# A two-block transformer step: Bst written in pieces from ScalarE's queue, constants moved, heads and skip later, zero products, four last pieces

## The chip, the cores and the metric

The kernel runs on one core of a Trainium2 chip. The metric is the device time of one execution in microseconds (us). One core has TensorE (PE, matrix products; PEld is its weight load), VectorE (DVE), ScalarE (ACT), GpSimd (POOL) and SyncE (SP), which here only issues DMA transfers. Each engine works through its own instructions in order; ACTq, SPq and POOLq are DMA issues from ScalarE, SyncE and GpSimd.

## What is computed

256 tokens of width 1024 go through two blocks. The first has two layers of attention (three kinds of heads) and a feed-forward part gated by a convolution over three tokens. The second runs a state-space scan (S5) and a sparse attention side by side, and then a product-key layer over 128 x 128 experts.

```
for layer in range(2):
    h = rms_norm(x, g_mix[layer])
    mix = concat(differential, moba, dilated attention of h @ w_in[layer])
    x = x + mix @ w_out[layer]
    u = causal_conv3(rms_norm(x, g_ffn[layer]) @ w_up[layer]) + conv_b
    gate, val = split(u)
    x = x + (silu(gate) * val) @ w_down[layer]
h = rms_norm(x, g_final)
proj = rmsnorm(h) @ w_in_2
y_ssm = gelu(real(C @ scan(a_bar, b_bar @ u)) + d_skip * u), then gated by w_glu
y_attn = softmax over the 64 keys that the index scores select
h = h + (sigmoid(g_ssm) * y_ssm @ w_ssm_up + sigmoid(g_attn) * y_attn @ w_attn_up) @ w_out
out = rmsnorm(h + experts(rmsnorm(h)))
```

## The kernel before

All large weights are cut into 515 tiles of 128 x 1024 numbers (512 KB each), and the class Weights (line 66) streams them. load_to issues a tile's transfer on SyncE's queue into one of four raw buffers. split_to cuts it into two parts, whi by ScalarE (line 94) and wlo = raw - whi by VectorE, now and then by GpSimd (line 96). TensorE makes three passes of each product from them (mm3: lines 156 and 159). There are six buffers for parts, and the splits run up to four tiles ahead.

The order of the work is written out by hand. Small work on ScalarE and VectorE is put off with w.post and issued by the next w.flush, which every request for a tile ends with, so that a posted step stands behind the splits of that request:

```
self.load_to(i + n + self.ahead)
self.split_to(...)
self.flush()
```

**Start.** build (line 1968) loads x and the first tiles on SyncE's queue. setup1 (line 333) loads five constants (mask_ab, masks, lamv, gd, cw) on GpSimd's queue; they are first used by the softmax steps from line 384 and the convolution. x is transposed on TensorE against the identity (line 217); ScalarE and VectorE evacuate it as hTh and hTl (lines 226, 228).

**Feed-forward part.** For each of 22 column blocks, j = 0 to 21, conv (line 774) runs on ScalarE (line 780) and VectorE (line 783) from a PSUM bank; tanh (line 790) follows on ScalarE, gated and split make gh and gl on VectorE, GpSimd and ScalarE (lines 796 to 804), each one flush later. Six blocks later down multiplies gh and gl with w_down. For j < 2 and for the last four blocks tanh is called at once, for the others it is posted.

**Beside it, in layer 0,** s5_b prepares the S5 tables as a generator that advances a step at a time between products. It makes BB on GpSimd, transposes it in eight groups of four (line 1020) into PSUM banks, posts eight evacuations into Bst (128 x 4096) on ScalarE, shown as L108, and writes all of Bst, 2 MB, to memory with one transfer on SyncE's queue (line 1026). Block 2 reads it back much later.

**Block 2.** A table plan, filled by at(m, step), says at which step m of the product loop each part is issued. UNITS gives m for the scores of the eight attention heads; the softmax (self.s3: VectorE lines 384 and 387, ScalarE line 390, TensorE line 399) follows two steps later, and values one more. The top-64 selection runs on VectorE before it (lines 1234 to 1239). scan is pushed through 11 levels on GpSimd and one on VectorE (lines 1269 to 1272); scan_end is a last push on VectorE. skip (line 1295, GpSimd) makes z = u * d_skip, which y_mm and gelu1 use from step 24 on. It is asked for at step 9.

**End.** The last products come out by columns of 128 in the order 4, 5, 0, 1, 2, 3, 6, 7. Each pair is copied by VectorE and ScalarE (lines 1944, 1946), and turn (line 1918) transposes it back one pair later; when a piece, (4, 6), (0, 4) or (6, 8), is complete, VectorE adds the residual (line 1931), ScalarE squares it and GpSimd scales it. Then come the sum of squares, the root and the output.

## Time and profile before

| what | value |
|---|---|
| median of 3 runs | 1671.91 us (1670.87 to 1672.17) |
| profiled execution | 1672.08 us, span 1670.0 us |
| mean granted clock of TensorE in the span | 0.988 of full speed |
| TensorE busy | 1616.1 us, 97% of the span |
| VectorE busy | 1299.8 us, 78% |
| ScalarE busy | 845.9 us, 51% |
| GpSimd busy | 699.0 us, 42% |
| moved by DMA | 328.49 MB, 197 GB/s in the mean |

The span runs from the first to the last instruction of the profiled execution; 2.1 us of its time lie outside it. A timeline row gives the start, the time, the engine, the line of the kernel, the operation, out<-in by the program's names with partitions x elements, and a count where like instructions in a row are drawn together; in brackets stands how long the engine had been idle before and what ended that. A matmul's time includes its way through the array, so that times of neighbours overlap. In the windows the clock is a share of 2.4 GHz, so 0.5 is the level of 1.2 GHz.

### The profile page before, as it was taken

How to read it: one execution, taken by the hardware profiler on the slowest of the kernel's cores; microseconds unless marked ns; L12 is line 12 of the kernel's file. 1: busy time of each engine (PE TensorE's matmuls, PEld its weight loads, DVE VectorE, ACT ScalarE, POOL GpSimd, SP SyncE). 2: the span in 40 equal slices, each digit the busy share in tenths (PEclk: the TensorE clock that was granted, in tenths of full speed). 3: DMA queues.
4: the chain of work that ended last, by engine and by line, in shares of the span. 5: the costliest groups of instructions: out<-in, count | busy, mean ns of one | idle time of the engine just before them, and what ended most of it. 6: DMA issues, size and time to landing. Idle time of an engine off the chain costs nothing.

```text
span 1670.0 us, 31715 instructions
## 1 busy us (share of the span) xinstructions
PE 1616.1 (97%) x12410; PEld 1476.5 (88%) x12410; DVE 1299.8 (78%) x2318; ACT 845.9 (51%) x1308; POOL 699.0 (42%) x610
## 2 busy tenths in 40 slices
PE   8999999889999999997999999999999999999996
PEld 6788999767889998775879999999999999999996
DVE  6775997666769866787663899889999889877775
ACT  6555655455556454643445545544444444455553
POOL 2313529322148933673020454323343222277773
PEclk9999999989999999998999999999999999999998
DMA  7435565464356557823356455777777655689982
GB/s 248 143 122 169 166 188 177 165 205 131 107 187 195 184 162 252 305 77 126 101 171 217 159 177 194 247 228 262 254 258 251 207 178 181 195 291 302 305 301 77
DMA packets 94325, 328.49 MB, mean 197 GB/s; under 512 B 11920, under 2 KB 16176, under 8 KB 93280
## 3 DMA queue, kind: packets, MB, share of 16 engines
q1 hardware_dynamic: 82992, 285.27, 51.1%
q0 software_dynamic: 10176, 39.03, 7.4%
q10 hardware_dynamic: 1008, 2.17, 0.4%
q8 instruction: 97, 1.59, 0.4%
q14 instruction: 52, 0.43, 0.1%
HBM read 318.57 MB, written 7.47 MB: 195 GB/s over the span
## 4 chain that ended last, share of the span: by engine, by line
PE 82%; DVE 8%; ACT 3%; DMA 3%; issue 2%; POOL 1%; ACTq 0%; SPq 0%; POOLq 0%; DVEq 0%
PE side L159 19%; PE acc L159 15%; PE side L156 10%; PE acc L156 8%; PE acc L1884 7%; PE acc L1877 6%; PE acc L1882 3%; PE acc L1879 3%; DVE wlo L96 3%; DMA raw<-in_ws 3%; PE side L1757 2%; ACT whi L94 1%; PE side L399 1%; PE side L376 1%; PE side L375 1%
## 5 line engine op out<-in xcount | busy, mean ns | idle before, releaser
L96 DVE TENSOR_TENSOR wlo<-raw,whi 128x1024 fp32r<-128x1024 f32 x462 | 609.2, 1330 | 221.0 <-ACT whi L94 220.3
L94 ACT ACTIVATE whi<-raw 128x1024 fp32r<-128x1024 f32 x511 | 535.8, 1057 | 456.1 <-PE acc L1882 174.0
L159 PE MATMUL side<-hTh,wlo 128*128 128x224 f32 (+1 forms) x1664 | 224.4, 277 | 2.8 <-DVE wlo L96 2.5
L156 PE MATMUL side<-hTh,whi 128*128 128x224 f32 (+1 forms) x1664 | 225.5, 278 | 0.8 <-ACT Bst L108 0.8
L159 PE MATMUL side<-hTl,whi 128*128 128x224 f32 (+1 forms) x1664 | 223.6, 277 | 0.0
L156 PEld LDWEIGHTS side<-hTh,whi 128*128 128x128 f32 x1664 | 207.6, 191 | 4.0 <-ACT Bst L108 1.1
L159 PEld LDWEIGHTS side<-hTh,wlo 128*128 128x128 f32 x1664 | 205.7, 191 | 3.9 <-DVE wlo L96 3.3
L159 PEld LDWEIGHTS side<-hTl,whi 128*128 128x128 f32 x1664 | 205.9, 191 | 0.0
L96 POOL TENSOR_TENSOR wlo<-raw,whi 128x1024 fp32r<-128x1024 f32 x49 | 125.9, 2572 | 178.2 <-ACT whi L94 170.9
L1847 POOL TENSOR_TENSOR ahl<-S,ahl 128x224 fp32r<-128x224 f32 x125 | 123.4, 988 | 173.8 <-ACT ahl L1846 173.2
L1884 PE MATMUL acc<-ahl,wlo 128*128 128x224 f32 x992 | 130.9, 274 | 0.0
L156 PE MATMUL acc<-whi,hTh 128*128 128x512 f32 x384 | 124.2, 416 | 1.3 <-ACT whi L94 1.3
L1877 PE MATMUL acc<-ahl,whi 128*128 128x448 f32 x496 | 124.4, 372 | 0.7 <-ACT S L1772 0.7
L1884 PEld LDWEIGHTS acc<-ahl,wlo 128*128 128x128 f32 x992 | 120.7, 192 | 0.0
L159 PE MATMUL acc<-wlo,hTh 128*128 128x512 f32 x384 | 117.9, 400 | 1.2 <-DVE wlo L96 1.1
L159 PE MATMUL acc<-whi,hTl 128*128 128x512 f32 x384 | 117.9, 399 | 0.3 <-DVE hTl L222 0.3
L159 PEld LDWEIGHTS acc<-wlo,hTh 128*128 128x128 f32 x384 | 72.7, 190 | 20.7 <-DVE wlo L96 3.2
L797 POOL TENSOR_TENSOR th<-th,cv 128x256 f32<-128x256 f32 x44 | 47.6, 1082 | 103.0 <-DVE th L796 99.6
L783 DVE SCALAR_TENSOR_TENSOR cv<-side,cw,cv 128x254 f32<-128x254 f32 (+1 forms) x176 | 72.5, 472 | 22.3 <-ACT cv L780 22.3
L159 PEld LDWEIGHTS acc<-whi,hTl 128*128 128x128 f32 x384 | 72.9, 190 | 18.3 <-DVE hTl L222 0.8
L1877 PEld LDWEIGHTS acc<-ahl,whi 128*128 128x128 f32 x496 | 84.3, 190 | 5.2 <-issue 1.4
L1696 POOL DMA_INDIRECT rows<-in_un,eid x32 | 47.0, 1470 | 96.4 <-DVE rows L1705 94.3
(487 smaller groups left out, 2787.7 us busy)
## 6 DMA issues: line engine op xcount, KB each, us to landing
raw<-in_ws SPq DMA_DIRECT2D x259, 512.0 KB, 4.0
raw<-in_us SPq DMA_DIRECT2D x128, 512.0 KB, 3.9
raw<-in_vs SPq DMA_DIRECT2D x128, 512.0 KB, 4.2
dBst<-Bst SPq DMA_DIRECT2D x1, 2048.0 KB, 7.4
dCT<-CT SPq DMA_DIRECT2D x2, 1024.0 KB, 7.9
tg<-dBst POOLq DMA_DIRECT2D x1, 2048.0 KB, 9.4
gb<-in_g_ffn SPq DMA_DIRECT2D x2, 512.0 KB, 5.3
s5bc<-in_s5bc SPq DMA_DIRECT2D x2, 512.0 KB, 5.8
```

The source lines that it names most:

```text
L94: self.nc.scalar.activation(hi, t, AF.Copy)
L96: eng.tensor_tensor(lo, t, hi.bitcast(FT), op=OP.subtract)
L156: mm(ps, sh, mh, start=first, stop=False)
L159: mm(ps, sl if side == "s" else sh, ml if side == "m" else mh, start=False, stop=last and side == late)
L783: nc.vector.scalar_tensor_tensor(o[which][:, n:], p[which][:, :S - n], cw[which][:, 2 - n:3 - n], o[which][:, n:], op0=OP.mult, op1=OP.add)
L797: nc.gpsimd.tensor_tensor(th, th, o[1], op=OP.mult)
L1696: G.indirect_dma_start(out=r, out_offset=None, in_=table, in_offset=bass.IndirectOffsetOnAxis(ap=eid[:, n:n + 1], axis=0))
L1847: G.tensor_tensor(al, src, ah.bitcast(FT), op=OP.subtract)
L1877: mm(acc[k][:, 0:2 * N], wts[i][0][:, s], A[i], start=first, stop=False)
L1879: mm(column(k), wts[i][0][:, s], A[i][:, 0:N], start=first and k % 2 == 0, stop=False)
L1882: mm(column(k), wts[i][0][:, s], A[i][:, N:2 * N], start=False, stop=False)
L1884: mm(column(k), wts[i][1][:, s], A[i][:, 0:N], start=False, stop=last and i == len(A) - 1 and (k < 4 or k % 2 == 1))
```

## The change

- UNITS is raised, so that the heads of block 2 come up to two steps later.
- The five constants of setup1 are issued on ScalarE's queue.
- idle makes products of zeros with no reader: ten before the first transposes, three behind the first evacuation.
- In the feed-forward part tanh is posted for the last four blocks too, in both layers.
- Each evacuation of Bst is followed on ScalarE by the transfer of its 256 KB; the transfer of 2 MB on SyncE's queue is gone.
- skip is asked for at step 12.
- The last columns are turned in four pieces of two, in the midst of the next pair's products, and three of the four sums of squares are added up ahead of the last.

```diff
-UNITS = (20, 20, 21, 22.5, 23, 23.5, 24, 25)
+UNITS = (21.5, 22, 22.5, 23, 23.5, 24, 24.5, 25)
...
     def setup1(self):
         self.mask_ab = self.b1c.tile([128, 384], FT, name="mask_ab")
-        nc.gpsimd.dma_start(out=self.mask_ab, in_=a["masks"][:, 0])
+        nc.scalar.dma_start(out=self.mask_ab, in_=a["masks"][:, 0])
         msk = c.tile([128, 2, 384], FT, name="masks")
-        nc.gpsimd.dma_start(out=msk, in_=a["masks"][:, 1:3])
+        nc.scalar.dma_start(out=msk, in_=a["masks"][:, 1:3])
...
         lamv = c.tile([128, 2, 4, 32], FT, name="lamv")
         gd = c.tile([128, 2, 64], FT, name="gd")
         cw = c.tile([128, 2, 44, 4], FT, name="cw")
...
+    def idle(self, n):
+        ps = self.acc.tile([128, 512], FT, name="acc")
+        for _ in range(n):
+            self.nc.tensor.matmul(ps, self.zero[:, 0:128], self.zero, start=True, stop=True)
...
-            if j < 2 or j >= NJ - 4:
+            if j < 2:
                 tanh(j, o)
             else:
                 w.post(tanh, j, o)
...
+        def put(dst, ps, at):
+            nc.scalar.activation(dst, ps.rearrange("p (a b) -> p a b", b=128), AF.Copy)
+            nc.scalar.dma_start(out=self.spill["Bst"][:, at:at + 512], in_=dst.rearrange("p g m -> p (g m)"))
+
         for i in range(8):
...
-            self.w.post(nc.scalar.activation, Bst[:, ri, gp], ps.rearrange("p (a b) -> p a b", b=128), AF.Copy)
+            self.w.post(put, Bst[:, ri, gp], ps, 2048 * ri + 512 * h)
             yield
             if i in (0, 1, 7):
                 yield
-        nc.sync.dma_start(out=self.spill["Bst"], in_=Bst.rearrange("p r g m -> p (r g m)"))
...
-        at(9, skip)
+        at(12, skip)
...
-        pieces = [(4, 6), (0, 4), (6, 8)]
+        pieces = [(4, 6), (0, 2), (2, 4), (6, 8)]
...
             for k in ks:
                 v_mm(124, A, wts, [k], True)
+                if b and k % 2 == 0:
+                    turn(order[2 * b - 2])
+                    turn(order[2 * b - 1])
+            if b == 3:
+                V.scalar_tensor_tensor(v, ms[:, :, 0], EPS, ms[:, :, 1], op0=OP.add, op1=OP.add)
+                V.tensor_tensor(v, v, ms[:, :, 2], op=OP.add)
...
-            for k in order[2 * b - 2:2 * b] if b else ():
-                turn(k)
         turn(6)
         turn(7)
-        V.scalar_tensor_tensor(v, ms[:, :, 0], EPS, ms[:, :, 1], op0=OP.add, op1=OP.add)
-        V.tensor_tensor(v, v, ms[:, :, 2], op=OP.add)
+        V.tensor_tensor(v, v, ms[:, :, 3], op=OP.add)
...
+                zero = self.zero = self.tiny.tile([128, 512], BF, name="zero", bufs=1)
+                nc.vector.memset(zero, 0.0)
+                self.idle(10)
...
                 self.h_ready(0)
+                self.idle(3)
```

Three places show how the instructions stand. First ScalarE's order at the end of layer 0, before. Here cv, th and gh are the steps of a column block (line 780, 792, 803), whi a split, L108 the evacuation of Bst:

```order
L94 ACTIVATE whi<-raw 128x1024 x2
L803 ACTIVATE gh<-th 128x256
L780 ACTIVATE cv_3723<-side,cw 128x256
L780 ACTIVATE cv_3725<-side,cw 128x256
L792 ACTIVATE th<-cv_3723 128x256
L108 ACTIVATE Bst<-side 128x512 x2
L94 ACTIVATE whi<-raw 128x1024
L108 ACTIVATE Bst<-side 128x512 x2
L94 ACTIVATE whi<-raw 128x1024
L108 ACTIVATE Bst<-side 128x512
L94 ACTIVATE whi<-raw 128x1024 x2
L803 ACTIVATE gh<-th 128x256
```

and in the change, the same stretch (line numbers are shifted; DMA dBst is a piece's transfer):

```order
L94 ACTIVATE whi<-raw 128x1024 x2
L786 ACTIVATE cv_3741<-side,cw 128x256
L786 ACTIVATE cv_3743<-side,cw 128x256
L1023 ACTIVATE Bst<-side 128x512
L1024 DMA dBst<-Bst 128x512
L1023 ACTIVATE Bst<-side 128x512
L1024 DMA dBst<-Bst 128x512
L94 ACTIVATE whi<-raw 128x1024
L809 ACTIVATE gh<-th 128x256
L798 ACTIVATE th<-cv_3741 128x256
L1023 ACTIVATE Bst<-side 128x512
L1024 DMA dBst<-Bst 128x512
```

The two convolution steps no longer stand behind gh, tanh has moved from before the evacuations to behind the next gh, and each evacuation is followed by its transfer. On SyncE's queue the tiles now follow each other with no transfer of Bst between.

Second VectorE's order in block 2, from the last step of the selection (msel) to the first softmax step (L384), before:

```order
L1239 SCALAR_TENSOR_TENSOR msel<-msel,mask_ab 128x384
L96 TENSOR_TENSOR wlo<-raw,whi 128x1024 x2
L1269 TENSOR_TENSOR ya<-st,ap 128x480
L1270 TENSOR_TENSOR ya<-st,ap 128x480
L1271 TENSOR_TENSOR ya<-ya 128x480
L1272 TENSOR_TENSOR st<-st,ya 128x15x32
L96 TENSOR_TENSOR wlo<-raw,whi 128x1024
L384 ISA sm,mx<-side,msel 128x128
```

and in the change:

```order
L1249 SCALAR_TENSOR_TENSOR msel<-msel,mask_ab 128x384
L96 TENSOR_TENSOR wlo<-raw,whi 128x1024 x2
L1279 TENSOR_TENSOR ya<-st,ap 128x480
L1280 TENSOR_TENSOR ya<-st,ap 128x480
L1281 TENSOR_TENSOR ya<-ya 128x480
L1282 TENSOR_TENSOR st<-st,ya 128x15x32
L96 TENSOR_TENSOR wlo<-raw,whi 128x1024 x3
L390 ISA sm,mx<-side,msel 128x128
```

Three splits stand ahead of the first softmax step behind scan_end, where one stood.

Third ScalarE's queue at the start, between the evacuation of the second half of x and the first roots, before:

```order
L194 ACTIVATE squares,ms<-x 128x512 x2
L226 ACTIVATE hTh<-side,g_93 128x128 x8
L94 ACTIVATE whi<-raw 128x1024 x5
L194 ACTIVATE squares,ms<-x 128x512 x2
L280 ACT_TABLE_LOAD
L280 ACTIVATE sincos<-sc_r 128x48
```

and in the change:

```order
L194 ACTIVATE squares,ms<-x 128x512 x2
L226 ACTIVATE hTh<-side,g_106 128x128 x8
L94 ACTIVATE whi<-raw 128x1024 x4
L336 DMA mask_ab<-in_masks 128x384
L338 DMA masks<-in_masks 128x768
L342 DMA lamv<-in_lam 128x256
L346 DMA gd<-in_g_diff 128x128
L349 DMA cw<-in_conv 128x2x176
L94 ACTIVATE whi<-raw 128x1024
L194 ACTIVATE squares,ms<-x 128x512 x2
```

The five constants stand between the fourth and the fifth of these splits. On GpSimd they are gone.

## Rows read from the trace of the kernel before

**Rows 1.** The page: busy time of each engine, share of the span, instructions.
```profile
PE 1616.1 (97%) x12410; PEld 1476.5 (88%) x12410; DVE 1299.8 (78%) x2318; ACT 845.9 (51%) x1308; POOL 699.0 (42%) x610
```

**Rows 2.** Waits of TensorE over the whole span: total, times, longest.
```profile
PE side L399 <- ACT sm L390: 10.8, 1, 10.8
PE acc L156 <- ACT gh L803: 6.4, 1, 6.4
PE side L217 <- DMA ident<-in_ident: 5.4, 1, 5.4
PE side L1020 <- ACT th L792: 3.4, 1, 3.4
...
PE side L156 <- ACT Bst L108: 0.8, 1, 0.8
```

**Rows 3.** Windows: length, busy PE, PEld, DVE, ACT, POOL, PE clock, DMA share, GB/s.
```profile
5.00:15.30 10.30, 8.47 (x23) 6.12 (x24) 5.56 (x11) 5.12 (x11) 1.23 (x2) 1.00 1.02 359
```

**Rows 4.** Timeline of the first 30 us, TensorE, then ScalarE and its queue (ACTq).
```profile
14.44 1.01 PE L156 MATMUL acc<-whi,hTh 128*128 128x512 f32 x2
...
18.75 0.63 PE L156 MATMUL acc<-whi,hTh 128*128 128x512 f32 x2
19.21 0.62 PE L159 MATMUL acc<-wlo,hTh 128*128 128x512 f32 x2
...
0.90 0.38 ACTq L1984 DMA_DIRECT2D g<-in_g_col  x1
...
15.34 1.06 ACT L94 ACTIVATE whi<-raw 128x1024 fp32r<-128x1024 f32 x1 [3.53 <-DMA raw<-in_ws]
...
25.61 1.06 ACT L94 ACTIVATE whi<-raw 128x1024 fp32r<-128x1024 f32 x1 [2.00 <-DMA raw<-in_ws]
```

**Rows 5.** Windows around the last five transpose groups of layer 0, same columns.
```profile
316.70:320.20 3.50, 0.07 (x2) 0.07 (x2) 3.01 (x5) 1.80 (x5) 1.41 (x2) 0.84 0.28 111
320.20:326.00 5.80, 5.80 (x16) 4.70 (x17) 3.15 (x3) 3.77 (x6) 0.72 (x1) 0.51 0.00 0
333.00:339.30 6.30, 0.00 (x0) 0.00 (x0) 1.54 (x2) 2.42 (x3) 0.00 (x0) 0.75 0.86 337
339.30:346.50 7.20, 6.44 (x15) 4.74 (x16) 2.99 (x4) 1.45 (x4) 2.75 (x2) 0.51 0.49 147
```

**Rows 6.** Timeline of that stretch: ScalarE, VectorE, SyncE's queue.
```profile
317.01 0.42 ACT L803 ACTIVATE gh<-th 128x256 fp32r<-128x256 f32 x1 [0.96 <-POOL th L797]
...
336.57 1.06 ACT L94 ACTIVATE whi<-raw 128x1024 fp32r<-128x1024 f32 x1 [9.29 <-DMA raw<-in_ws]
...
315.18 2.88 DVE L96 TENSOR_TENSOR wlo<-raw,whi 128x1024 fp32r<-128x1024 f32 x2
318.37 1.65 DVE L783 SCALAR_TENSOR_TENSOR cv<-side,cw,cv 128x255 f32<-128x255 f32 x4 [0.31 <-ACT cv L780]
...
307.02 8.26 SPq L83 DMA_DIRECT2D raw<-in_ws  x4
327.31 0.33 SPq L1026 DMA_DIRECT2D dBst<-Bst  x1
327.76 12.81 SPq L83 DMA_DIRECT2D raw<-in_ws  x6
```

**Rows 7.** The page's DMA issues: KB each, us from issue to landing.
```profile
raw<-in_ws SPq DMA_DIRECT2D x259, 512.0 KB, 4.0
...
dBst<-Bst SPq DMA_DIRECT2D x1, 2048.0 KB, 7.4
```

**Rows 8.** Timeline of block 2 before the attention heads: GpSimd, then VectorE.
```profile
709.23 2.99 POOL L1295 TENSOR_TENSOR z<-u,s5d 128x1024 f32<-128x1024 f32 x1
...
762.01 4.47 DVE L96 TENSOR_TENSOR wlo<-raw,whi 128x1024 fp32r<-128x1024 f32 x2
```

**Rows 9.** Timeline of the last 15 us: TensorE, then ScalarE.
```profile
1659.35 0.53 PE L1924 MATMUL side<-ident,rows 128*96 128x128 f32 x3 [0.27 <-DVE hTh L1931]
...
1661.19 0.19 ACT L1932 ACTIVATION_READ_ACCUMULATOR S<-hTh 128x1 f32 x1
```

More of the change, by code (lines that the diff above doesn't have):

```diff
@@ L341, in setup1 @@
         lsrc = a["lam"]
-        nc.gpsimd.dma_start(out=lamv.rearrange("p a b c -> p (a b c)"),
+        nc.scalar.dma_start(out=lamv.rearrange("p a b c -> p (a b c)"),
                             in_=bass.AP(tensor=lsrc.tensor, offset=lsrc.offset, ap=[[0, 128], [1, 256]]))
@@ L345, in setup1 @@
         gsrc = a["g_diff"]
-        nc.gpsimd.dma_start(out=gd.rearrange("p a b -> p (a b)"),
+        nc.scalar.dma_start(out=gd.rearrange("p a b -> p (a b)"),
                             in_=bass.AP(tensor=gsrc.tensor, offset=gsrc.offset, ap=[[0, 128], [1, 128]]))
         cw = c.tile([128, 2, 44, 4], FT, name="cw")
-        nc.gpsimd.dma_start(out=cw.rearrange("p l a b -> p l (a b)"), in_=a["conv"].rearrange("l p n -> p l n"))
+        nc.scalar.dma_start(out=cw.rearrange("p l a b -> p l (a b)"), in_=a["conv"].rearrange("l p n -> p l n"))
         self.cw = cw
@@ L1913, in peer @@
         xg = [self.raw.tile([128, D], FT, name="raw") for _ in range(2)]
-        ms = self.tiny.tile([128, 2, 3], FT, name="ms3")
-        pieces = [(4, 6), (0, 4), (6, 8)]
+        ms = self.tiny.tile([128, 2, 4], FT, name="ms3")
+        v = self.tiny.tile([128, 2], FT, name="vars")
+        pieces = [(4, 6), (0, 2), (2, 4), (6, 8)]
         tok = [slice(0, 128), slice(0, N - 128)]
         def turn(k):
-            i = [k0 <= k < k1 for k0, k1 in pieces].index(True)
+            i = pieces.index((k // 2 * 2, k // 2 * 2 + 2))
             k0, k1 = pieces[i]
@@ L1948, in peer @@
                     V.tensor_tensor(dst, acc[k][:, N:2 * N], dst, op=OP.add)
-            for k in order[2 * b - 2:2 * b] if b else ():
-                turn(k)
         turn(6)
         turn(7)
-        v = self.tiny.tile([128, 2], FT, name="vars")
-        V.scalar_tensor_tensor(v, ms[:, :, 0], EPS, ms[:, :, 1], op0=OP.add, op1=OP.add)
-        V.tensor_tensor(v, v, ms[:, :, 2], op=OP.add)
+        V.tensor_tensor(v, v, ms[:, :, 3], op=OP.add)
         r = self.rsqrt(v, 2)
```

## The prediction

> **What bounds the kernel now.** I read the page first, then TensorE's waits, then windows over the stretches where it waited, then the timelines there. The page shows TensorE busy 97% of the span [rows 1]. So the other engines' loads matter only where TensorE stands still or runs at half its clock, and 1670.0 less 1616.1 leaves 53.9 us of standing still. The waits name the large pieces [rows 2]: 10.8 us for the first softmax of block 2, 6.4 us for gh at the end of layer 0, 5.4 us for the identity at the very start, 3.4 us at a transpose at the end of layer 0; outside that list stands the tail, where only the other engines work. The change touches all five. None of its parts removes TensorE work worth counting; it adds 13 small products and reorders the rest.
>
> Standing still has a second price. In the windows the granted clock is 0.51 while TensorE works off what a wait left behind [rows 5], which is the 1.2 GHz level in place of 2.4 GHz; a pair of 512-column products that lasts 0.63 us at full speed lasts 1.01 us [rows 4].
>
> **Head: constants and zero products, 2.0 us gained (0 to 2.7).** Up to 15.3 us the DMA share is 1.02 at 359 GB/s [rows 3], so what lands is a matter of bytes. ScalarE waits 3.53 us for the fourth weight tile and starts on it at 15.34 [rows 4]; TensorE can't go on without it. The five constants are 966,656 bytes by the shapes in the diff. Behind four more splits they no longer stand ahead of that tile: 0.967 MB / 359 GB/s = 2.7 us. That is the upper end. But up to 14.44 us TensorE is at the low level [rows 4], and would still be working through the first three tiles when the fourth lands at about 12.6; only the zero products, by bringing the clock up before the first transposes, let both come together. Neither part alone does much: zero products alone meet the same late tile, so I cost them at 0 by themselves. They run in the 5.4 us in which TensorE waits for the identity [rows 2]: ten single products of 0.23 us (half the 0.46 us from one pair to the next at full speed [rows 4]) at 0.51 of the clock are 4.5 us, which ends about when the identity lands; if the cover is too short, some tenths of delay. I take 2.0, because the transposes of the second token block and their evacuation don't shrink with the bytes. The lower end, 0, is that the constants give back later what they took. Their five issues at 0.38 us each [rows 4] are 1.9 us on ScalarE, in front of a split that now waits 2.00 us for its tile [rows 4]: hidden, unless the tile comes earlier by more than that. Their bytes now share with tiles that TensorE has several products in hand for.
>
> **End of layer 0: 13.5 us gained (5 to 15).** The 2 MB table Bst now leaves SyncE's queue with one transfer at 327.31, after the last evacuation; the queue had issued its last tile by 315.3 and six tiles stand behind the table [rows 6]. Their buffers came free with the splits that end at 318.06 [rows 6], so they waited 9.7 us for order alone. The first then lands so late that ScalarE waits 9.29 us for it, to 336.57 [rows 6]; gh stands behind that split on ScalarE, and TensorE behind gh. With the table in eight pieces on ScalarE's queue, tiles go out near 317 and 318 and land 4.0 us later [rows 7], ahead of the splits that want them. From the last transposes TensorE then has the work between 326.0 and 333.0 (the edges of windows in rows 5), 7 us; ScalarE needs one evacuation 0.6, one issue 0.4, two splits 2.1 and gh 0.4, together 3.5 us. So gh is there 3.5 us ahead, and the following subtraction on GpSimd too. Terms:
> - the wait for gh and the short one behind it: 6.3 + (7.20 - 6.44) = 7.1 us [rows 5];
> - the low clock behind it: 6.44 x (1 - 0.51) = 3.2 us [rows 5];
> - the wait of 0.8 us for an evacuation of Bst [rows 2], which now comes ahead of a split: 0.8 us;
> - the wait of 3.4 us at the seventh transposes [rows 2]: it ends with tanh of the last column block, behind gh at 317.01 and VectorE's four steps at 318.37 [rows 6]. With tanh posted, these steps still follow two splits that end at 318.06, so they can't move far; I keep 2.4 us of it and count 1.0;
> - the low clock behind that, (1 - 0.51) x 5.80 = 2.8 us [rows 5]. The clock of 0.84 over that wait means that it fell about 2.3 us in (0.32 of 3.5 us at half). [...]
> Together 13.5. With that clock kept it is 14.9, without 12.1. Against it stand eight issues of 0.38, 3.0 us of ScalarE in a stretch where it is busy about 3.8 of 5.8 us [rows 5]; if they fall where TensorE waits for a split, the gain sinks to about 5 (below).
>
> What decides at this place is the order of issue, not bandwidth: between 320.2 and 326.0 the DMA share is 0.00 while buffers are free [rows 5]. The Trainium skill speaks against both queue moves: "DMA: Bandwidth & Descriptors", section "Issuing engines are not separate DMA queues", says that transfers run on the same 16 engines whoever issues them, and that another issuer saves only the sequencer's issue time. By it the moves would save that time, 0.3 us, and the waits would stay; that case is the rival on the table's bytes.
>
> **Attention heads and skip: 1.2 us gained (-0.4 to 2.7).** The first pair of heads goes from 20 to 21.5 and 22, so at least 1.5 steps of the plan, six product pairs each, come ahead of the wait for the softmax: 1.5 x 6 x 0.46 us [rows 4] = 4.1 us. But VectorE has no idle time there, and its order now has two more splits ahead of the first softmax step: 2.88 us for two [rows 6]. Net 1.2. If only one of them delays the softmax it is 2.7. Against it, skip (2.99 us on GpSimd [rows 8]) now runs just behind the scan, beside VectorE's scan_end. What that costs is bounded by the two splits that ran beside the scan, 4.47 us [rows 8] against 2.88: 1.6 us at most, which makes -0.4. Skip's old place was already in GpSimd's idle time, so moving it saves nothing. I take 1.2, since VectorE's small steps are short beside a split. Most of the 10.8 us remains: the softmax still waits for VectorE.
>
> **Tanh in layer 1: 0.** The same chain there ended without a wait in TensorE's list [rows 2].
>
> **Last columns: 0.8 us gained (0.4 to 1.3).** Now the transposes of the last columns wait 0.27 us for VectorE and end near 1659.9, and ScalarE's squares run without a break until 1661.38 [rows 9]. In four pieces the last transposes start right behind their evacuation and only two narrow squares are left. Four earlier transposes move ahead of the last products (+0.4), the two wide squares and the wait fall off the path (-1.2).
>
> **Sum.** 2.0 + 13.5 + 0 + 1.2 + 0.8 = 17.5 us. The profiled execution took 1672.08 (span 1670.0), which gives 1654.6; the runs' median is 1671.91, 0.2 lower, which gives 1654.4. A measurement of this kernel tells a difference of about 0.2% (3.3 us) from none.
>
> **Rivals.**
> - *ScalarE becomes late at the end of layer 0.* Three microseconds of issues stand between evacuations and splits, each split feeds TensorE, and the wait for gh comes down only to 3.5 us with the low clock after it. The gain there is 13.5 - 3.5 - 3.2 - 1.4 = 5.4, the sum 9.4, the time 1662.5. For it: ScalarE is the engine that every wait there names. Against: the margin of 3.5 us. Chance 0.18.
> - *Head and heads give nothing.* The constants come back at 24 us on DMA engines that are still full, and take their 2.7 us from the tiles of the next products; skip costs VectorE all of the 1.6 us. Then 13.5 + 0.8 - 0.4 = 13.9, and 1658. Chance 0.17.
> - *Zero products raise nothing.* They end before the identity lands or leave the clock low; then the head gives some 0.5 in place of 2.0, and the time is 1656, inside the forecast's range.
> - *All upper ends:* clock kept at the seventh transposes, one split covered: 2.7 + 14.9 + 2.7 + 1.3 = 21.6, and 1650.3. Chance 0.05.
> - *The table's bytes hold the tiles back wherever they are issued.* The first tile behind the table landed near 336.5, 8.8 us after its issue, against 4.0 us for a tile at large [rows 6, 7], so sharing does slow it. If the pieces and the tiles share in the same way in the new place, for long enough to keep gh late, the 7.1 and 3.2 us stay: 17.5 - 10.3 = 7.2, and 1664.7. Against: 4.8 us more than 321 is 326, and gh 3.5 us later is still ahead of 333. Chance 0.03. (This is where the Trainium skill's rule, above, leads.)
> - *Slower: issues on ScalarE that block.* If each of the later seven issues has to wait for an earlier transfer's landing, 4.0 us [rows 7], ScalarE stands 28 us in a stretch of about 23, of which it now idles four tenths, some 9 us [rows 5]. TensorE then waits 19 us where it waits 3.4 + 7.1 now, so the end of layer 0 loses 8.5 in place of gaining 13.5: 17.5 - 13.5 - 8.5 = -4.5, and 1676. It decides from a mean wait of about 3.4 us for each issue. Against: the queue's issue at the start goes through in 0.38 us [rows 4], and the DMA engines are nearly idle there. Chance 0.05, of which 0.02 near the point that decides.
>
> **Chances.** Forecast 0.52; the rivals 0.18, 0.17, 0.05, 0.03 and 0.05. The range 1649 to 1664 takes in all but the last two. Faster by over 0.2%: 0.95; within: 0.02; slower: 0.03.
>
> **What would show it.** Right: no wait of TensorE for gh near 330, tiles issued by SyncE near 317, a clock of 1.00 through 330 to 345 in layer 0; the fourth tile's split near 12.7 and full-speed products before 10 us; a softmax wait in block 2 split in two and still 8 to 10 us in all; squares that end nearer to the last product. Wrong: ScalarE's queue standing at a piece of Bst, a wait for a split in front of a side product at 305 to 325, or a low clock that starts elsewhere.

## The result and the profile after

| | before | changed |
|---|---|---|
| median, six runs each | 1671.59 us (1668.09 to 1672.28) | 1650.8 us (1648.52 to 1660.29) |
| ratio to before, 95% interval | 1 | 0.9888 (0.9863 to 0.9913) |
| profiled execution, its span | 1672.08, 1670.0 us | 1649.52, 1647.6 us |
| mean granted clock in the span | 0.988 | 0.994 |

The change is faster by 20.8 us, or 1.1%. Forecast were 1654.4 us and a range of 1649 to 1664. Executions of the changed kernel spread further than those of before (the table's ranges), and the long ones show a lower mean clock, 0.990 against 0.995; where it fell in them is not shown. The mean clock and the busy time tell the same from two sides: on the page after, TensorE works 3.2 us less than before [rows 1] for 13 instructions more, and stands still for 34.7 us in place of 53.9.

```profile
PE 1612.9 (98%) x12423; PEld 1473.7 (89%) x12423; DVE 1296.5 (79%) x2322; ACT 846.9 (51%) x1312; POOL 697.4 (42%) x607
```

To see where the 22.4 us of the two spans came from, I cut each span at three places that every kernel here has: TensorE's transposes of the normalized rows (xn) of the second half of the tokens, ahead of the feed-forward part of layer 0, that of layer 1, and the experts. In the timeline of the changed kernel these are:

```profile
141.76 0.66 PE L217 MATMUL side<-ident,xn 128*128 128x128 f32 x4 [0.53 <-ACT xn L712]
...
460.20 0.66 PE L217 MATMUL side<-ident,xn 128*128 128x128 f32 x4 [0.52 <-ACT xn L712]
...
853.22 0.66 PE L217 MATMUL side<-ident,xn 128*128 128x128 f32 x4 [0.54 <-ACT xn L712]
```

The same rows of before start at 144.96, 481.54 and 876.65. The differences of these times are the lengths of the stages; the last column runs to the end of the span.

| kernel | to layer 0's feed-forward part | to layer 1's | to the experts | to the end | span |
|---|---|---|---|---|---|
| before | 144.96 | 336.58 | 395.11 | 793.35 | 1670.0 |
| changed | 141.76 | 318.44 | 393.02 | 794.38 | 1647.6 |
| difference | -3.2 | -18.1 | -2.1 | +1.0 | -22.4 |

The first stage holds the start, the second the end of layer 0, the third the attention heads of block 2, the fourth the tail. The profiles of the experiments below give the spread of a stage whose code is the same: 141.1 to 142.5 in the first, 318.15 to 318.7 in the second, 392.4 to 395.75 in the third, 792.5 to 795.3 in the fourth. So -2.1 in the third and +1.0 in the fourth are within what these stages vary by; the gains of the first and the second are beyond it, and most of the whole lies in the second.

TensorE's waits after (total, times, longest) no longer have gh, the transposes at the end of layer 0 and the evacuation of Bst [rows 2]. The wait for the identity is 0.2 in place of 5.4, with zero products running until then; that for the softmax is 2.8 in place of 10.8, with one of 2.5 for a split ahead of it (the longest in the first line). The 2.8 is one profile's: in the six others with the same steps in block 2 it is 0.3 to 5.4.

```profile
PE acc L159 <- DVE wlo L96: 5.7, 6, 2.5
...
PE side L405 <- ACT sm L396: 2.8, 1, 2.8
...
PE side L217 <- DMA ident<-in_ident: 0.2, 1, 0.2
```

Windows over the end of layer 0 (length, busy PE, PEld, DVE, ACT, POOL, PE clock, DMA share, GB/s) show 1.00 of the clock throughout, where rows 5 have 0.51 behind each wait, and a DMA share that never falls to 0.00:

```profile
300.00:310.00 10.00, 10.00 (x75) 9.35 (x74) 8.29 (x13) 8.52 (x14) 4.23 (x3) 1.00 0.82 278
310.00:320.00 10.00, 9.92 (x50) 7.96 (x49) 6.61 (x11) 7.99 (x14) 3.54 (x3) 1.00 0.98 338
320.00:330.00 10.00, 10.00 (x49) 8.14 (x48) 7.13 (x8) 5.64 (x10) 3.73 (x4) 1.00 0.66 211
```

The timeline there, ScalarE with its queue, then VectorE, then SyncE's queue:

```profile
310.39 1.00 ACT L786 ACTIVATE cv<-side,cw 128x256 f32<-128x256 f32 x2
311.28 0.59 ACT L1023 ACTIVATE Bst<-side 128x512 f32<-128x512 f32 x1
311.91 0.33 ACTq L1024 DMA_DIRECT2D dBst<-Bst  x1
312.28 0.60 ACT L1023 ACTIVATE Bst<-side 128x512 f32<-128x512 f32 x1 [0.40 <-ACT Bst L1023]
...
320.70 0.40 ACT L809 ACTIVATE gh<-th 128x256 fp32r<-128x256 f32 x1
...
312.06 1.64 DVE L789 SCALAR_TENSOR_TENSOR cv<-side,cw,cv 128x255 f32<-128x255 f32 x4
...
297.94 30.91 SPq L83 DMA_DIRECT2D raw<-in_ws  x13
```

A piece's issue takes 0.33 us and keeps ScalarE for 0.40 between two evacuations. SyncE's queue holds 13 tiles in a row with nothing between them. The last gh starts at 320.70 and TensorE has no wait for it. VectorE's four convolution steps (cv, L789) run at 312.06; before, the last ones ran at 318.37 [rows 6].

The start, TensorE, then ScalarE and its queue:

```profile
1.22 4.01 PE L376 MATMUL acc<-zero 128*128 128x512 bf16 x10 [1.22 <-DVE zero L1997]
...
8.27 0.73 PE L156 MATMUL acc<-whi,hTh 128*128 128x512 f32 x2
...
16.49 0.63 PE L156 MATMUL acc<-whi,hTh 128*128 128x512 f32 x2
...
12.42 1.06 ACT L94 ACTIVATE whi<-raw 128x1024 fp32r<-128x1024 f32 x1 [1.28 <-DMA raw<-in_ws]
...
19.56 0.34 ACTq L336 DMA_DIRECT2D mask_ab<-in_masks  x1
```

The ten zero products end just ahead of the identity, the first pair of weight products takes 0.73 us where pairs took 1.01 as late as 14.44 [rows 4], and the fourth split starts at 12.42 where it started at 15.34 [rows 4]. As a mark for the start I take the second whi pair behind the transposes of the second half of x: 16.49 here, 18.75 before [rows 4].

Block 2 ahead of the first softmax, TensorE, VectorE, GpSimd:

```profile
743.83 0.73 PE L159 MATMUL acc<-wlo,hTh 128*128 128x512 f32 x2 [2.50 <-DVE wlo L96]
...
753.80 0.84 PE L405 MATMUL side<-ident,sm 128*128 128x128 f32 x3 [2.84 <-ACT sm L396]
...
741.50 5.12 DVE L96 TENSOR_TENSOR wlo<-raw,whi 128x1024 fp32r<-128x1024 f32 x2
...
742.65 2.89 POOL L1305 TENSOR_TENSOR z<-u,s5d 128x1024 f32<-128x1024 f32 x1
```

The tail, TensorE's last product and the last transposes, which wait 0.89 us for the copies of its result:

```profile
1635.73 0.50 PE L1894 MATMUL acc<-S 128*128 128x224 f32 x3
1637.11 0.82 PE L1935 MATMUL side<-ident,rows 128*128 128x128 f32 x4 [0.89 <-DVE rows L1963]
```

From the last product's end (1636.23) to the span's end there are 11.4 us; before, the same stretch was 12.4 (1657.64 to 1670.0).

### The profile page after: what moved, and what is told of

Read it like the earlier page. It is cut to its first block, busy times and chain, and to the rows that moved or that the text cites. A ratio compares the mean times of both kernels' runs of the same rounds, so it can differ in the third digit from the quotient of the medians.

```text
span 1647.6 us, 31746 instructions
## 1 busy us (share of the span) xinstructions
PE 1612.9 (98%) x12423; PEld 1473.7 (89%) x12423; DVE 1296.5 (79%) x2322; ACT 846.9 (51%) x1312; POOL 697.4 (42%) x607
## 3 DMA queue, kind: packets, MB, share of 16 engines
q8 instruction: 97, 1.59, 0.4%
## 4 chain that ended last, share of the span: by engine, by line
PE 87%; DVE 4%; ACT 3%; DMA 2%; POOL 2%; issue 1%; ACTq 0%; DVEq 0%; POOLq 0%
PE side L159 22%; PE acc L159 16%; PE side L156 11%; PE acc L156 8%; PE acc L1894 7%; PE acc L1887 6%; PE acc L1892 3%; PE acc L1889 3%; PE side L1767 2%; DVE wlo L96 2%; DMA raw<-in_ws 1%; ACT whi L94 1%; PE side L405 1%; PE side L382 1%; PE side L381 1%
## 5 line engine op out<-in xcount | busy, mean ns | idle before, releaser
L96 DVE TENSOR_TENSOR wlo<-raw,whi 128x1024 fp32r<-128x1024 f32 x462 | 600.5, 1311 | 203.4 <-ACT whi L94 202.1
L789 DVE SCALAR_TENSOR_TENSOR cv<-side,cw,cv 128x254 f32<-128x254 f32 (+1 forms) x176 | 72.4, 472 | 21.5 <-ACT cv L786 21.5
```

Of the source, the lines that this page charges most:

```text
L96: eng.tensor_tensor(lo, t, hi.bitcast(FT), op=OP.subtract)
L789: nc.vector.scalar_tensor_tensor(o[which][:, n:], p[which][:, :S - n], cw[which][:, 2 - n:3 - n], o[which][:, n:], op0=OP.mult, op1=OP.add)
```

## The experiments

The theory: the second stage's 18.1 us come from two causes of about equal size, the table's place in the order of issue and tanh's place in ScalarE's order. The rivals: that the eight pieces do it by their size or early start, that bandwidth was short, that tanh is worth little, as forecast. For the other stages each part is undone alone.

**1. One transfer of 2 MB on SyncE's queue again**, rest as changed.

```diff
-            nc.scalar.dma_start(out=self.spill["Bst"][:, at:at + 512], in_=dst.rearrange("p g m -> p (g m)"))
...
+        nc.sync.dma_start(out=self.spill["Bst"], in_=Bst.rearrange("p r g m -> p (r g m)"))
```

> The changed kernel, but Bst leaves with one transfer of 2 MB on SyncE's queue at the end of the steps again. Theory (the order of issue held the tiles): the tiles of layer 0's end stand behind the table again, TensorE waits 4 to 8 us for gh and works the next 6 us at the low clock (3 us more), so 7 to 11 us slower than the changed kernel. Rival (the table's bytes share the 16 DMA engines wherever they are issued): within 2 us of the changed kernel, and no wait for gh.

Measured: 1659.41 us (1658.13 to 1660.6), ratio 0.9928 (0.9911 to 0.9944). The waits for gh (6.3) and gl (0.7) are back, the second stage is 328.13, 9.7 us longer. The timeline, SyncE's queue and ScalarE:

```profile
300.25 9.14 SPq L83 DMA_DIRECT2D raw<-in_ws  x5
316.85 0.33 SPq L1036 DMA_DIRECT2D dBst<-Bst  x1
317.30 12.79 SPq L83 DMA_DIRECT2D raw<-in_ws  x6
...
326.07 1.06 ACT L94 ACTIVATE whi<-raw 128x1024 fp32r<-128x1024 f32 x1 [9.24 <-DMA raw<-in_ws]
```

The queue issues its last tile by 309.4, then stands until the table goes at 316.85; the next tiles start at 317.30 and the split that needs the first waits 9.24 us for it (the bracket of 326.07). The low clock behind the wait is back too, in the window 328 to 336 (columns as in the windows above):

```profile
328.00:336.00 8.00, 6.42 (x16) 4.77 (x17) 3.69 (x5) 2.23 (x6) 2.76 (x2) 0.56 0.48 161
```

**2. One transfer of 2 MB, but on ScalarE's queue.** The same edit with nc.scalar for nc.sync.

> The changed kernel, but Bst leaves with one transfer of 2 MB on ScalarE's queue, after the last evacuation. Theory (order of issue): the tiles on SyncE's queue pass it, no wait for gh, within 1.5 us of the changed kernel. Rival (bytes): the tiles that go out from 319 us on land 4 to 5 us late, and TensorE waits 3 us or more there or just behind. If the pieces themselves matter (work for ScalarE in small steps), this kernel is faster by up to 1 us, since seven issues fall away.

Measured: 1650.25 us (1649.3 to 1662.94), 0.9908 (0.9874 to 0.9943); second stage 318.15, no wait for gh. Against experiment 1 only the queue differs, and the second stage is 10.0 us shorter; against the changed kernel only the pieces do, and it lies at the edge of the 318.2 to 318.7 of those with pieces. So the pieces don't matter, the queue does. The page's DMA issues (KB each, us from issue to landing) show that the table does share the DMA engines with the tiles:

```profile
dBst<-Bst ACTq DMA_DIRECT2D x1, 2048.0 KB, 9.9
```

It takes 9.9 us beside tiles where it took 7.4 [rows 7], and the tile issued at 318.97 landed 8.4 us later. Nobody waits for either.

**3. Tanh at once for the last four blocks again.**

```diff
-            if j < 2:
+            if j < 2 or j >= NJ - 4:
```

> The changed kernel, but tanh of the last four column blocks is called at once again in both layers. Theory: the wait at the seventh transposes hangs on the order in which tanh, the evacuations and VectorE's steps are asked for, so it comes back with 3 to 4 us, and the low clock behind it with 2 to 3 us: 5 to 7 us slower than the changed kernel. Rival (that wait went because the table and the queue went): no wait there, within 1 us. The prediction's own step (most of the wait is bound by VectorE's splits and stays) would have the two kernels differ by 1 to 2.4 us.

Measured: 1662.11 us (1658.81 to 1664.12), 0.9946 (0.9925 to 0.9967); second stage 326.21, 7.8 longer. TensorE waits 4.9 us at the seventh transposes, in two waits of 0.5 and 4.4 that the list puts down to tanh. ScalarE, VectorE, TensorE:

```profile
308.78 0.42 ACT L798 ACTIVATE th<-cv 128x256 f32<-128x256 f32 x1 [2.39 <-DVE cv L789]
...
314.26 1.00 ACT L786 ACTIVATE cv<-side,cw 128x256 f32<-128x256 f32 x2
317.63 0.42 ACT L798 ACTIVATE th<-cv 128x256 f32<-128x256 f32 x1 [2.37 <-DVE cv L789]
317.95 0.58 ACT L1023 ACTIVATE Bst<-side 128x512 f32<-128x512 f32 x1
...
316.29 1.64 DVE L789 SCALAR_TENSOR_TENSOR cv<-side,cw,cv 128x255 f32<-128x255 f32 x4
...
318.07 0.63 PE L1031 MATMUL side<-ident,BB 128*128 128x128 f32 x4 [4.37 <-ACT th L798]
```

ScalarE stands 2.39 us and then 2.37 us at tanh for VectorE's steps of the same block. What it has to do behind that, evacuations and splits and the next block's convolution, is late by as much: VectorE's last steps run at 316.29 in place of 312.06. The evacuation's wait of 0.8 is back, and the low clock (0.75 over 6.9 us from 318.1, 1.7 us) makes up nearly all of the rest of the 7.8. The medians differ by 11.3; what the second stage leaves lies in the third, 397.57 in this profile, where the clock is at 0.50 from 783.0 to 789.8.

The list names tanh because it ended last, but the times speak for VectorE. The transposes start 0.02 us behind tanh's end (318.05) and 0.14 behind the end of VectorE's fourth step (317.93); before, the second distance is 0.15 too (320.02 to 320.17). A wait for ScalarE alone ends 0.05 us behind it here. In five waits of other profiles, at the softmax's transposes, for both engines with ScalarE done 1.95 us earlier, TensorE starts 0.15 us behind VectorE's step. So TensorE waited for VectorE's four steps. Tanh, which needs the third of them, ends at nearly the same moment.

**4. The kernel before with tanh posted in layer 0 and 1, and nothing else.** The same line, the other way.

> The kernel before with one edit: tanh of the last four column blocks is posted. Theory (that edit alone takes the wait at the seventh transposes away): the waits of 0.8 and 3.4 us and the low clock of 2.8 us behind go, the wait for gh stays at 6 to 6.5 us with its low clock, so 6 to 8 us faster than before. Rival (it needs the pieces on ScalarE's queue as well): the wait of 3.4 us stays, within 2 us of before.

Measured: 1663.64 us (1661.42 to 1664.38), 0.995 (0.9933 to 0.9967); second stage 327.66, 8.9 shorter. The wait of 3.4 and the one of 0.8 for Bst are gone, the wait for gh stays at 6.4. The 8.9 of this run and the 9.7 of the first make 18.6, against 18.1 for the whole: two causes, nearly additive.

**5. No zero products**, the constants where the change has them.

```diff
-                self.idle(10)
...
-                self.idle(3)
```

> The changed kernel without the 13 products of zeros. Theory (zero products and constants only gain together): TensorE works up to 13 or 15 us at the low clock, the fourth tile is there near 12.4 us and waits for it; the first pass ends 1.5 to 2.2 us later, and so does everything. Rival 1 (zero products do nothing): within 0.5 us, clock low or not. Rival 2 (they are the whole gain of the head): 2.5 to 3 us slower.

Measured: 1653.16 us (1648.27 to 1658.58), 0.9906 (0.9882 to 0.993); first stage 143.09, 1.3 longer than changed. TensorE, then ScalarE:

```profile
13.99 1.05 PE L159 MATMUL acc<-whi,hTl 128*128 128x512 f32 x2
...
18.62 0.63 PE L156 MATMUL acc<-whi,hTh 128*128 128x512 f32 x2
...
9.88 3.05 ACT L94 ACTIVATE whi<-raw 128x1024 fp32r<-128x1024 f32 x3
```

The splits run without a wait, and TensorE is at the low level (1.05 us a pair) until 14.85: now TensorE is late, not the tile. Its mark stands at 18.62, 0.13 ahead of before. (In experiment 4, which has neither part, the clock rises by 12.2 all the same, TensorE then waits for the late tile, and the mark is 19.57.)

**6. The constants on GpSimd's queue again**, with the zero products (nc.gpsimd for nc.scalar in the five lines of setup1).

> The changed kernel with the five constants on GpSimd's queue at the start again. Theory: the fourth tile lands 2.5 to 2.9 us later, near 15.2 us, TensorE is warm but waits for it, 2.0 to 2.8 us slower, of which up to 1 us may come back because the tiles at 22 to 32 us no longer share with the constants. Rival (the constants only change places with later tiles): within 0.7 us.

Measured: 1653.93 us (1652.55 to 1655.74), 0.99 (0.9883 to 0.9917); first stage 144.13, 2.4 longer. TensorE's mark, and ScalarE's fourth split, late again:

```profile
18.70 0.62 PE L156 MATMUL acc<-whi,hTh 128*128 128x512 f32 x2
...
15.29 1.06 ACT L94 ACTIVATE whi<-raw 128x1024 fp32r<-128x1024 f32 x1 [3.37 <-DMA raw<-in_ws]
```

TensorE is at its full level and waits for the tile: 18.70, 0.05 ahead of before. In the ten profiles here that have both parts, the mark lies between 16.49 and 17.87, 17.17 in the mean; in the two that have neither, at 18.75 and 19.57 (before and experiment 4), 19.16 in the mean. So both together give 2.0 us, and neither alone, one profile each, comes near that; whether one alone gives nothing or half a microsecond, two profiles that differ by 0.8 can't tell. The change moves the constants in time and to another queue at once, and no run parts the two. The two latest marks with both parts (17.83 and 17.87, experiments 1 and 10) are those where the clock was at 0.5 from about 11 to 14 although the zero products had run. The stages show more (1.9 for constants alone, 0.8 for zeros alone, 3.2 for both), but that comes later: before waits twice, at 39 and 46 us, for a step on GpSimd (qkn), 1.2 us together; experiment 4, with the same code there, not at all, and the changed kernel once, 0.7.

**7. The old steps of the heads.**

```diff
-UNITS = (21.5, 22, 22.5, 23, 23.5, 24, 24.5, 25)
+UNITS = (20, 20, 21, 22.5, 23, 23.5, 24, 25)
```

> The changed kernel with UNITS as before. Theory: one wait of about 10 to 11 us for the softmax in place of 2.5 + 2.8 us and some clock, VectorE reaches the first softmax step two splits (2.5 us) earlier; 0.5 to 2 us slower. Rival (VectorE is the bound there, so the order of TensorE's work is worth nothing): within 0.5 us. Rival (the change cost something): up to 1 us faster.

Measured: 1652.41 us (1651.12 to 1653.62), 0.9889 (0.9873 to 0.9906); third stage 396.62, 3.6 longer and just outside the spread, in one profile each; the ratio, 0.9889 against 0.9888, shows no difference. The wait for the softmax is 12.5 in one piece, 1.7 more than before [rows 2], since skip now runs in it. VectorE, then GpSimd:

```profile
744.84 2.36 DVE L1279 TENSOR_TENSOR ya<-st,ap 128x480 f32<-128x480 f32 x1
747.12 0.65 DVE L1280 TENSOR_TENSOR ya<-st,ap 128x480 f32<-128x480 f32 x1
...
743.80 2.89 POOL L1305 TENSOR_TENSOR z<-u,s5d 128x1024 f32<-128x1024 f32 x1
```

Two like steps of scan_end, of one size (128x480), take 2.36 us beside skip and 0.65 behind it: 1.7 us, by as much as the wait is longer. The first step's end, 747.20, lies 0.5 us behind skip's (746.69).

**8. skip at step 9, as before; heads as changed** (at(9, skip) for at(12, skip)).

> The changed kernel with skip at step 9 again, in GpSimd's idle time ahead of the scan. Theory (skip beside VectorE's splits costs VectorE time): the two splits behind the selection take 4.0 to 4.6 us in place of 5.1, the wait for them 0.5 to 1 us less, and the whole is 0.3 to 1 us faster. Rival (skip ahead of the scan delays the scan): the scan starts up to 3 us later and the whole is 0.5 to 2 us slower. Rival (neither): within 0.3 us.

Measured: 1647.96 us (1645.99 to 1650.18), 0.9864 (0.9847 to 0.988); the lowest median here; third stage 391.29, 1.7 shorter and below the whole spread. TensorE's two waits, then the pair of splits in front of scan_end:

```profile
743.18 0.72 PE L159 MATMUL acc<-wlo,hTh 128*128 128x512 f32 x2 [1.38 <-DVE wlo L96]
...
752.51 0.84 PE L405 MATMUL side<-ident,sm 128*128 128x128 f32 x3 [3.73 <-ACT sm L396]
...
740.82 4.52 DVE L96 TENSOR_TENSOR wlo<-raw,whi 128x1024 fp32r<-128x1024 f32 x2
```

The pair takes 4.52 in place of 5.12 us, and ends 1.3 us earlier, 0.7 of it because it starts earlier. The intervals of this kernel and the changed one overlap in part, so by the times alone it isn't shown to be faster; its fastest run, its stage and the rows above point the same way.

**9. Three pieces at the end**, with the transposes behind the products again (pieces (4, 6), (0, 4), (6, 8); sums added up at the end).

> The changed kernel with the last columns turned in the three old pieces. Theory: between TensorE's last product and the end of the span lie 12.4 us as in the kernel before, in place of 11.4, and TensorE reaches its last product 0.35 us earlier, since four transposes no longer stand ahead of it: 0.6 us slower in all, which a timing of this kernel can't tell but the trace can. Rival (the four narrow pieces cost as much as they save): the same span from the last product but one to the end, within 0.2 us.

Measured: 1651.88 us (1649.92 to 1659.16), 0.9889 (0.9857 to 0.9921). TensorE's last products:

```profile
1638.44 0.50 PE L1894 MATMUL acc<-S 128*128 128x224 f32 x3
```

From the last product's end, 1638.94, to the span's end, 1651.6, there are 12.7 us, against 11.4: 1.3 in that profile, 1.0 against before. The stretch is 11.3 to 11.4 in every profile with four pieces and 12.4 to 12.7 in the three with the old ones. Four transposes that now stand ahead of the last products take back 0.36 (in the changed kernel, from 1634.29 to the next product at 1634.65), so 0.6 to 0.9 remain. The runs' times can't show so little.

**10 to 12. Can more be had in block 2?** All three keep skip at step 9. Two give splits of VectorE to GpSimd, so that VectorE reaches the softmax sooner: every second split from step 19 to 23, or all from 19 to 22.

```diff
+        at(19, setattr, w, "share", 2)
+        at(23, setattr, w, "share", 0)
```

> The changed kernel with skip at step 9 again, and every second split of the steps 19 to 22 of block 2 made by GpSimd, which is idle there once the scan is done. Theory (VectorE bounds the first softmax): of five splits behind the selection VectorE makes three, the waits of 1.4 and 3.7 us with skip at step 9 shrink to 2 to 3 us in all, 1 to 3 us faster than with skip at step 9 alone. Rival (GpSimd's splits, 2.6 us each and slower beside VectorE, are late themselves): TensorE waits for GpSimd's wlo instead, within 0.5 us or slower.

> As the kernel before in this list, but all splits of the steps 19 to 21 go to GpSimd. Theory: VectorE reaches the softmax one split (1.2 us) earlier still, but GpSimd now makes three splits in a row at 2.6 us and more, and TensorE waits for the second or third: 0 to 2 us slower than with every second split. Rival (GpSimd keeps up): 0.5 to 1.5 us faster than that.

Measured: 1653.93 us (1652.02 to 1655.57) and 1656.84 us (1651.75 to 1664.52). Neither brought a gain, and the theory behind both failed. The first is slower than its base, experiment 8, as its rival had it, but not by TensorE waiting for GpSimd's splits: its softmax transposes start 2.5 us later (755.01 against 752.51). The second's executions overlap with the first's, so which of the two is slower is not shown. VectorE, then GpSimd, of the first:

```profile
744.56 2.80 DVE L1279 TENSOR_TENSOR ya<-st,ap 128x480 f32<-128x480 f32 x1
...
743.51 6.08 POOL L96 TENSOR_TENSOR wlo<-raw,whi 128x1024 fp32r<-128x1024 f32 x2
```

Beside GpSimd's subtractions VectorE's steps take 2.80 us in place of 0.65. What VectorE was spared it lost here, and more.

The third fills the wait for the softmax with zero products, to hold the clock:

```diff
+        at(23.5, self.idle, 14)
```

> The changed kernel with skip at step 9, and 14 more products of zeros on TensorE just ahead of the first softmax transposes of block 2 (3.0 us at full speed, in a wait of 3.7 us). Theory (the slower executions of the changed kernel are those in which the clock falls in block 2's waits and stays low): the clock stays at full speed behind that wait, 1.0 to 2.0 us faster than with skip at step 9 alone, and the executions lie within 3 us of each other. Rival (the clock falls whatever stands in that wait, or the waits ahead of it decide): low clock behind 753 us as before, spread of 4 us and more, within 0.5 us or slower by what the products cost.

Measured: 1650.94 us (1650.29 to 1652.46), 0.988 (0.9864 to 0.9897). The zero products (14 in the edit, 13 in the trace) fill the wait and the clock is 1.00 behind it, but it falls at 773.2, in a stretch where TensorE is busy 9.26 of 10 us, and is 0.50 from 775 to 785, where it is busy all the time:

```profile
755.00:765.00 10.00, 10.00 (x64) 7.97 (x63) 2.80 (x17) 4.95 (x12) 0.00 (x0) 1.00 0.17 54
765.00:775.00 10.00, 9.26 (x65) 8.42 (x65) 4.90 (x12) 2.85 (x5) 0.00 (x0) 0.91 0.21 61
775.00:785.00 10.00, 10.00 (x38) 8.93 (x38) 6.49 (x12) 1.75 (x3) 0.00 (x0) 0.50 0.13 47
```

The executions lie within 2.2 us of each other, as expected; a gain over the kernel without them (1647.96) did not come.

## Why the prediction was right, step by step

The time came inside the range, 1654.4 against 1650.8, and the sign and most of the mechanism were right. But 1650.8 lies nearest to the rival "All upper ends" (1650.3, chance 0.05), and one of its conditions, the clock kept at the seventh transposes, came true. By spans the sum was 17.5 and 22.4 came; nearly all of the missing 4.9 is one term, the end of layer 0, and it is the width of the range that kept the time inside. The terms:

**Head: 2.0 forecast; at the mark 2.3 measured in that profile, 2.0 between the means.** The arithmetic of bytes held: the tile was forecast at about 12.6, and its split starts at 12.42. So did "neither part alone does much", as far as one profile each can tell: 0.13 and 0.05 against before (experiments 5 and 6), about half a microsecond against the mean of the two without either. The stage as a whole is 3.2 shorter; 0.5 of the rest is the waits for qkn, which come and go between profiles.

**End of layer 0: 13.5 forecast, 18.1 measured, beyond the 15 that I had set as its end.** The half on the table was right in mechanism and size: 7.1 + 3.2 = 10.3 forecast, 9.7 measured by putting it back (10.0 between experiments 1 and 2). The step that failed is the one on tanh: "With tanh posted, these steps still follow two splits that end at 318.06, so they can't move far; I keep 2.4 us of it and count 1.0", and one half, 1.4, of the clock behind it. The three terms on it, 0.8 + 1.0 + 1.4, made 3.2; experiments 3 and 4 show 7.8 and 8.9. No run shows a half of the clock's term: behind the seventh transposes the clock is low before (2.8 us) and in experiment 3 (1.7 us), and full in the changed kernel and in experiment 4. The wait of 3.4 us went whole, too. What I overlooked stands in ScalarE's order. Each tanh that is called at once holds ScalarE until VectorE has done its block's four steps, 1.4 to 2.4 us a block, and everything behind it moves back, the next block's convolution with it. The rows of before said so. VectorE's steps at 318.37 wait 0.31 us for ScalarE's convolution [rows 6], and the splits in front of them begin with a wait of 1.59 us for ScalarE, which had stood 1.39 us at the tanh before (311.81):

```profile
313.70 1.22 DVE L96 TENSOR_TENSOR wlo<-raw,whi 128x1024 fp32r<-128x1024 f32 x1 [1.59 <-ACT whi L94]
```

So "these steps still follow two splits" took for fixed what came late by the same chain. A second hold fell with the new order: gh, in front of the convolution before, kept ScalarE 0.96 us for GpSimd [rows 6]. The prediction's "it ends with tanh" is not right either: the wait ended with VectorE's four steps (experiment 3). Why the seventh transposes need not wait for VectorE at all now is not settled. In the instruction lists they wait for ScalarE and VectorE before and in experiment 3, for ScalarE alone in the changed kernel and in experiment 4; which PSUM bank they take in each is open.

**Heads and skip: 1.2 net forecast, 2.1 measured**, in a stage that varies by 3.3. Undone alone, in one profile each, the heads' new steps are worth 3.6 (4.1 was my count of the products moved ahead; the runs' times show no difference) and skip's new place costs 1.7. Neither is clear of that spread by much. I had named 1.6 as its bound and then took nearly nothing, "since VectorE's small steps are short beside a split". In experiment 7 just such a step costs 1.7. In the changed kernel skip meets the two splits ahead of scan_end (742.65 to 745.54), not its small steps as I had it, and the pair takes 5.12 us where it takes 4.52 in experiment 8. I had expected a softmax wait "still 8 to 10 us in all"; it is 2.5 + 2.8 = 5.3 in this profile, and its second part varies from 0.3 to 5.4.

**Tanh in layer 1: 0 forecast.** Put into the kernel before (experiment 4), it changes nothing there: third stage 394.90 against 395.11. Taken out of the changed one (experiment 3), TensorE is 1.4 us late at the end of layer 1, in one profile, with a wait of 0.7 for gl that the changed kernel hasn't. So 0 was right for the kernel that I read it from, and perhaps a microsecond short for the changed one.

**Last columns: 0.8 forecast, 0.6 to 0.9 measured.** The fourth stage grew by 1.0 all the same: in that one profile TensorE waits 1.0 us for a GpSimd step among the experts (ahl), which no part of the change touches.

**The rivals.** Issues that block did not come: each takes 0.33 to 0.35 us. ScalarE is not late at the end of layer 0. Sharing of bandwidth is there (9.9 against 7.4 us) but meets no one who waits. The Trainium skill ("DMA: Bandwidth & Descriptors", section "Issuing engines are not separate DMA queues") says that another issuer saves the sequencer's time alone. The shared engines show in this case's traces; that nothing else is saved does not hold here. Issue takes 0.33 us, and the move from one engine's queue to another's is worth 10.0 us of the stage (experiment 1 against experiment 2, which differ in nothing else), because transfers on one engine's queue go out in order and the tiles stood behind one that waited for its data.

## What to carry to other kernels

Look in each issue queue for a transfer whose data come late: what stands behind it waits for order alone, and moving it to another engine's queue was worth the wait and the low clock behind that here, though its bytes stayed the same. On an engine that works in order, an instruction that needs another engine's fresh result is put one round later, so that what is ready goes first. The row of an idle engine names what came last; follow that engine's own waits back from there, since the work that happens to lie in front of a step may be late by the same chain. Before small steps of VectorE are laid beside GpSimd's large ones, look for a row that shows the two together.

## What was not expected of the hardware

- VectorE's two-input step on 128x480 numbers takes 0.65 us alone and 2.36 to 2.82 us beside a GpSimd step on 128x1024 (experiments 7, 10 and 11), a factor of four. The pair of splits ahead of scan_end takes 4.5 beside the scan (before [rows 8] and experiment 8) and 5.1 beside skip; a pair at the end of layer 0 takes 2.88 [rows 6]. All six slow steps end 0.51 to 0.52 us behind the end of the GpSimd instruction that they met, as in experiment 7 (746.69 and 747.20): they look held until it is done, rather than slowed throughout.
- The clock can stay low, or fall, while TensorE is busy. In experiment 12 it falls at 773.2, with TensorE busy 9.26 of the 10 us around that, and is 0.50 in the next 10, with TensorE busy 10.00 (rows there). In experiment 11, in its longest execution, it is low behind a softmax wait of 4.1 us and stays so for 30 us, TensorE at 10.00 and 9.26 of 10. That stretch holds the scan's small products of 63 and 64 columns.

```profile
755.00:765.00 10.00, 10.00 (x34) 7.52 (x33) 3.93 (x17) 5.41 (x12) 0.00 (x0) 0.51 0.25 88
...
775.00:785.00 10.00, 9.26 (x37) 8.13 (x36) 2.11 (x9) 0.81 (x3) 0.00 (x0) 0.50 0.17 52
```
